# DeltaNet outputs taken by channel with one joint factor, and VectorE's long background operations in pieces, in one hybrid decoder layer

## The chip, the cores and the metric

The kernel runs on one core of one Trainium2 chip. The metric is the device time of one execution, in microseconds (us). Before the change the median of three runs is 1189.47 us (1189.45 to 1190.11).

## The reference: what is computed

One layer over 1024 tokens of width 1024, all in float32. After an RMSNorm one input projection makes the columns of two mixers:

```python
# mixer A, gated DeltaNet: 4 heads of 128; q, k, v pass a causal conv and SiLU, q and k are L2-normed
qa = l2norm(qa) * (GDN_HEAD_DIM ** -0.5)
def step(state, xs):                       # one chunk
    uv, wk, qd, at, ke, ge = xs
    u = uv - wk @ state
    o = qd @ state + at @ u                # qd = gam * q, gam = exp(cumulated log decay)
    state = ge * state + ke.T @ u
    return state, o
o_a = rmsnorm(o_a, gdn_norm_w) * silu(z)   # per token and head, over its 128 channels
# mixer B, dilated attention: 8 heads of 64, three strided bands merged by their softmax denominators
o_b = dilated_attention(qb, kb, vb)
x = x + concat(o_a, o_b) @ w_out
# then RMSNorm, an up-projection to 2 x 2816 columns, conv of width 3, SiLU gate, down-projection, RMSNorm
```

L2-norm and per-token RMSNorm both carry an epsilon of 1e-6. Both scale a token's 128 channels of a head by one number, so the scale of q need not be applied where a normalisation of the output follows, if the epsilon is treated accordingly.

## The kernel before

Activations lie channel by token: 128 channels on the partitions, 1024 tokens in the free dimension. A float32 product is made of three TensorE products of rounded high and low parts (`mm3`: high x high, high x low, low x high, 512 columns each); weights are loaded in tiles of 128x1024 (`wst`), and ScalarE makes the high part (`whi`), VectorE the low part (`wlo`, one operation of 1024 columns).

The program is one list per engine. TensorE's order is fixed when the program is built, by the class `Weave`: streams of work (generators) are started in order of a level, each says how long it must wait by a small cost model, and every matmul gets an order token. The other engines' orders come from a scheduler that follows the dependencies; operations issued through `uv` and `ua` (line 141 in the profile) are put ahead of those through `ve` and `ac` (line 139). Products carry line 192, transposes lines 196 and 201. All engines run their list in order, and DMAs are issued from SP's list, also in order.

The stages, with the times of the profiled execution:

- 0 to 186 us: the first projection columns, norms, and from `dense()` the columns q and v of the four heads (48 products of 512 columns for one column block). For each head `kprep` and `qprep` prepare the chunks. `qprep` transposes qT on TensorE (`tokens`: 8 transposes a head, into PSUM), ScalarE squares each transposed block with an accumulated sum per token (`ssq`), GpSimd raises it to -1/2 (`rq`), and VectorE makes `gq` = gam times rq. VectorE also runs `forward_sub`, the inverses of 32x32 blocks, 31 dependent steps from about 114 to 178 us, whose result goes through DRAM (`xdram`, `xtdram`) to `merges`.
- 186 to 226 us: `merges` joins the inverses to 128x128 blocks, with column blocks of `dense()` between.
- 226 to 303 us: the chain. For each of 4 heads and 8 chunks: product k x state (`ps<-ct,kT`), VectorE makes `r`; product with the inverse (`ps<-r,um`), VectorE makes `wke`, ScalarE `w`; product `ps<-wke,ktok`, VectorE makes the next state `ct`. Then the outputs: `ps<-ct,qat` (q x state) and `ps<-w,qat` (at x w) go token by channel to two halves of a PSUM bank, ScalarE copies one with the scale rq into `vtok`, VectorE adds the other with the scale gq, ScalarE squares the 128x128 block with an accumulated sum `ms`. At a head's end GpSimd raises `ms` to -1/2 and multiplies the 128x1024 `vtok` by it, and `finish(h)` transposes it back on TensorE (8 transposes) and stores it to `mixer`. The heads run interleaved; products of `dense()` (columns of the attention's q, k, v) fill the time between.
- 303 to 460 us: the attention, 4 pairs of heads, again with `dense()` between (the rest of the attention's columns, then the columns z, whose SiLU gates the DeltaNet output `og`, read back from `mixer`).
- 460 to 1188 us: out projection, up-projection, down-projection.

VectorE's operations of `dense()` in the chain and the attention are the eviction of a half column (`aqkv<-ps,rstdB`, 512 columns), the low part of a weight (`wlo<-wst,whi`, 1024 columns) and the 32x32-block transpose of V (`avt<-aqkv`, 1024 columns). Each is one instruction that lies somewhere between the chain's.

Of the kernel before, what the change touches and what calls it, by code (L numbers as in the profile page):

```python
# [7 lines left out]
F32 = mybir.dt.float32  # L8
# [7 lines left out]
P = 128  # L16
# [29 lines left out]
class Weave:  # L46
# [50 lines left out]

    def until(self, name):
        while name not in self.done:
            yield 0.3  # L100
# [20 lines left out]
class Engine:  # L121
# [5 lines left out]
    def __getattr__(self, op):  # L127
        wv, eng, name, fixed, per, lag, first = self.args

        def call(*a, **kw):  # L130
# [9 lines left out]
            with first(offset=URGENT):  # L140
                return getattr(eng, op)(*a, **kw)  # L141
# [3 lines left out]
def hybrid_layer(tc, I, out):  # L145
# [44 lines left out]

    def mm(dst, lhs, rhs, us, start=True, stop=True, **kw):
        tc.stamp_issue_order_token(nc.tensor.matmul(dst, lhs, rhs, start=start, stop=stop, **kw).ins, TOKEN)  # L192
        wv.product(us, dst, lhs, rhs)
# [27 lines left out]
    def weight(src, n=1024, st=None):  # L221
# [4 lines left out]
        lows_made.append(split(st, hi, lo))  # L226
        return hi, lo

    def wk(src, st=None):
        return [t.rearrange("p (k m) -> p k m", k=KT) for t in weight(src, st=st)]  # L230
# [16 lines left out]
    gdram = dp.tile([NCH * H, P], F32, name="gdram")  # L247
    xdram = dp.tile([H, 32, 1024], F32, name="xdram")
# [95 lines left out]
    pick = const("pick", [P, 32])  # L344
    ve.memset(pick, 0.0)
    ve.memset(pick[:, 8:9], 1.0)
# [64 lines left out]
    def gates():  # L411
# [25 lines left out]
        sy.dma_start(gdram, grow)  # L437
        ve.tensor_copy(gc, pt[:, :NCH * H].rearrange("p (c h) -> p c h", c=NCH))
# [5 lines left out]
    def scaled(pair, name, by_class=False, tag="ev", t=None, hs=(0, 1)):  # L444
        if t is None:
            t = A(name, tag)
        for h in hs:
            sl = half(h)
            if by_class:
                ve.tensor_tensor(t[:, sl].rearrange("p (n c u) -> p n u c", n=4, c=4),  # L450
                                        pair[h].rearrange("p (n u c) -> p n u c", n=4, c=4),
                                        rstdB[:, sl].rearrange("p (n u c) -> p n u c", n=4, c=4), op=OP.mult)
# [31 lines left out]
    def gate(og, xr, anchor=None):  # L484
# [3 lines left out]
                 ve.tensor_tensor(og, og, y, op=OP.mult)]  # L488
# [10 lines left out]
    gated = {}  # L499

# [7 lines left out]
    def dense():  # L508
# [7 lines left out]
        raw.append(raw_weight(I["wi"][1]))  # L516
        for i, col in enumerate(DENSE):
# [3 lines left out]
            w = nxt  # L521
            if i + 1 < len(DENSE):
                nxt = wk(None, raw.pop())
# [3 lines left out]
            for hh in range(2):  # L527
                pt = bank("hf")
                yield wv.need(pt, *w)
                for k in range(KT):  # L530
                    mm3(pt, [t[:, k, :] for t in w], [t[:, half(hh)] for t in xs[k]], k == 0, k == KT - 1)
                    yield 0.0

                pair.append(pt)
                if hh == 0:
                    while put_off:
# [12 lines left out]
            elif kind == "z":  # L549
                og = gated[h] = A("og", "kT*")  # L550
                sy.dma_start(og, mixer[h])
                if i + 1 < len(DENSE):
# [3 lines left out]
            else:  # L556
                if col[2] < 2:
                    sy.dma_start(apark[h, col[2]], xr)
                else:
                    t = A("avt", "ev")  # L560
                    ve.transpose(t.rearrange("p (c n j) -> p n c j", c=4, n=NCH), by_block(xr))
                    for b in range(4):
                        sq_.dma_start(avdram[h].rearrange("u x (b j) -> b u x j", b=4)[b],
                                     t[32 * b:32 * b + 32].rearrange("u (x j) -> u x j", j=32))
                wv.done.add(col)
# [20 lines left out]

    def kprep(h):
# [8 lines left out]
        rows = gdram.rearrange("(c h) t -> h c t", h=H)[h]  # L596
        sy.dma_start(v8(dec), bass.AP(tensor=rows.tensor, offset=rows.offset, ap=[[0, P]] + list(rows.ap)))
# [43 lines left out]
    def qprep(h, qT):  # L641
# [3 lines left out]
        ssq = small("ssq")  # L645
        yield from tokens(qT, None, None, ssq)
        ve.tensor_scalar(ssq, ssq, 128.0, 128.0 * EPS, op0=OP.mult, op1=OP.add)
        rq = small("rq", 4)
        rsqrt(rq, ssq, NCH)
# [11 lines left out]
        gq = small("gq", 4)  # L661
# [1126 lines left out]
```

## Time and profile before

| quantity | value |
|---|---|
| median of three runs | 1189.47 us |
| the profiled execution's own time | 1189.92 us |
| its span in the trace | 1188.1 us |
| share of the span that TensorE is busy | 99% |
| share of the span that VectorE is busy | 81% |
| TensorE's idle time, 226 to 303 us (chain) | 1.41 us of 77.00 |
| TensorE's idle time, 303 to 460 us (attention) | 0.39 us of 157.00 |

The span is 1.8 us shorter than the execution's own time; that remainder is taken as unchanged. A row of the timeline gives the start in us, the duration in us, the engine, the line, the operation, the tile written and those read, the size, and in brackets how long the engine had been idle before it and what ended that. Float32 products stand as two records each, transposes as one. Records of TensorE overlap, so the time that an instruction takes is read from one start to the next.

### The profile page before, as it was taken

Reading aid. Unit: us, or ns where it says so; the run is one execution under the profiler, and the core shown is the slowest. Engines: PE = TensorE matmul, PEld = TensorE weight load, DVE = VectorE, ACT = ScalarE, POOL = GpSimd, SP = SyncE. Lnnn points to the kernel's source line nnn. Section 1 sums busy time; section 2 is a strip of 40 time slices with the busy share of each in tenths; the row PEclk is TensorE's granted clock in tenths of the full one; section 3 lists DMA queues with packets and bytes.
Section 4 is the critical chain, followed back from the end, with each engine's and each line's share of the span. In section 5 each row is a group of like instructions: output and inputs, shape, how many; then the busy total and the mean of one; then the engine's idle time right before and its main releaser. Section 6 shows DMA issues by size and latency. Waiting matters only on the chain.

```text
span 1188.1 us, 18252 instructions
## 1 busy us (share of the span) xinstructions
PE 1178.3 (99%) x6994; PEld 975.0 (82%) x6994; DVE 964.0 (81%) x1545; ACT 572.8 (48%) x1122; POOL 54.7 (5%) x49
## 2 busy tenths in 40 slices
PE   9999999999999999999999999999999999999997
PEld 7888888898777778888888888888888888888887
DVE  7786996474577877668998898988889889898987
ACT  7473344364344444545544444545444553546452
POOL 0212001004000000000000000000000000000001
PEclk9999999999999999999999999999999999999999
DMA  7323456727642314443231313122231395356724
GB/s 238 108 94 86 110 141 161 238 96 204 180 141 73 99 37 151 150 151 107 89 99 61 107 54 107 60 100 89 72 106 54 124 379 196 125 178 221 239 96 160
DMA packets 114520, 156.91 MB, mean 132 GB/s; under 512 B 54368, under 2 KB 65408, under 8 KB 114432
## 3 DMA queue, kind: packets, MB, share of 16 engines
q1 hardware_dynamic: 113712, 155.21, 41.3%
q8 instruction: 55, 0.90, 0.3%
q10 hardware_dynamic: 720, 0.53, 0.1%
q14 instruction: 33, 0.27, 0.1%
HBM read 117.68 MB, written 38.03 MB: 131 GB/s over the span
## 4 chain that ended last, share of the span: by engine, by line
PE 98%; DVE 1%; ACT 0%; issue 0%; DVEq 0%; ACTq 0%
PE ps L192 47%; PE pa L192 20%; PE dw L192 18%; PE pc L192 10%; PE ps L201 1%; PE ps L196 1%; PE warm L192 0%; DVE x1h L139 0%; ACT sm L141 0%; PE pd L192 0%; DVE aqkv L139 0%; DVE sm L141 0%; DVE wke L141 0%; DVE xr L139 0%; DVE ct L141 0%
## 5 line engine op out<-in xcount | busy, mean ns | idle before, releaser
L192 PE MATMUL dw<-pr 128*128 128x512 f32 (+1 forms) x984 | 211.4, 377 | 0.0
L192 PEld LDWEIGHTS dw<-pr 128*128 128x128 f32 x984 | 176.7, 188 | 33.7
L192 PE MATMUL ps<-xhi,whi 128*128 128x512 f32 x448 | 184.0, 411 | 0.0
L192 PE MATMUL ps<-xhi,wlo 128*128 128x512 f32 x448 | 175.4, 392 | 0.0
L192 PE MATMUL ps<-xlo,whi 128*128 128x512 f32 x448 | 175.2, 391 | 0.0
L192 PE MATMUL pa<-T,pair 128*128 128x512 f32 x528 | 126.9, 389 | 0.0
L192 PEld LDWEIGHTS pa<-T,pair 128*128 128x128 f32 x528 | 99.1, 188 | 20.6
L192 PEld LDWEIGHTS ps<-xhi,whi 128*128 128x128 f32 x448 | 84.6, 189 | 18.8 <-issue 2.7
L192 PEld LDWEIGHTS ps<-xhi,wlo 128*128 128x128 f32 x448 | 84.3, 188 | 18.2
L192 PEld LDWEIGHTS ps<-xlo,whi 128*128 128x128 f32 x448 | 84.6, 189 | 14.6
L139 ACT ACTIVATE u<-pa 128x512 f32<-128x512 f32 x44 | 26.4, 599 | 114.4 <-PE pa L192 114.4
L139 DVE SCALAR_TENSOR_TENSOR y<-xu,fcw,y 128x1023 f32<-128x1023 f32 (+1 forms) x44 | 56.4, 1281 | 22.1 <-ACT y L139 22.0
L139 ACT ACTIVATE pr<-wd 128x1024 fp32r<-128x1024 f32 x33 | 35.0, 1061 | 72.6 <-DVE wd L139 35.4
L192 PE MATMUL pa<-B,A 128*128 128x512 f32 x264 | 63.5, 390 | 0.0
L192 PE MATMUL pc<-B,pair 128*128 128x512 f32 x264 | 63.4, 389 | 0.0
L192 PE MATMUL pc<-T,S 128*128 128x512 f32 x264 | 63.4, 389 | 0.0
L192 PE MATMUL pa<-T,S 128*128 128x512 f32 x264 | 63.4, 389 | 0.0
L139 ACT ACTIVATE whi<-wst 128x1024 fp32r<-128x1024 f32 (+2 forms) x38 | 38.5, 1013 | 51.1 <-PE ps L192 44.4
L139 DVE TENSOR_TENSOR wst<-wst 128x512 f32<-128x512 f32 x88 | 60.4, 687 | 0.8
L192 PE MATMUL ps<-B,pair 128*128 128x512 f32 x252 | 60.5, 389 | 0.0
L192 PEld LDWEIGHTS pc<-T,S 128*128 128x128 f32 x264 | 49.6, 188 | 10.3
L192 PEld LDWEIGHTS pa<-T,S 128*128 128x128 f32 x264 | 49.6, 188 | 10.3
(248 smaller groups left out, 2217.2 us busy)
## 6 DMA issues: line engine op xcount, KB each, us to landing
wst<-in_wu SPq DMA_DIRECT2D x44, 512.0 KB, 3.6
wd<-in_wd SPq DMA_DIRECT2D x44, 512.0 KB, 4.5
wst<-in_wi SPq DMA_DIRECT2D x25, 512.0 KB, 4.1
upark<-y SPq DMA_DIRECT2D x22, 512.0 KB, 3.5
r<-upark SPq DMA_DIRECT2D x22, 512.0 KB, 10.3
wa<-in_wd SPq DMA_DIRECT2D x22, 256.0 KB, 2.9
apark<-aqkv SPq DMA_DIRECT2D x8, 512.0 KB, 3.3
wst<-in_wo SPq DMA_DIRECT2D x8, 512.0 KB, 3.6
```

The costliest lines, as they stand in the source:

```text
L139: return getattr(eng, op)(*a, **kw)
L192: tc.stamp_issue_order_token(nc.tensor.matmul(dst, lhs, rhs, start=start, stop=stop, **kw).ins, TOKEN)
L196: tc.stamp_issue_order_token(nc.tensor.transpose(dst, src, ident).ins, TOKEN)
L201: tc.stamp_issue_order_token(nc.tensor.transpose(dst, src[rows], ident[rows, rows]).ins, TOKEN)
```

## The change

Four parts:

1. The chain's outputs are computed by channel: `ps<-qat,ct` and `ps<-qat,w` accumulate in one 128x128 PSUM tile (the operands change places), one ScalarE copy puts it into `vtok`, which is now channel by token. The scales rq and gq, the blockwise squares, `ms` with its powers, GpSimd's multiply, the 32 transposes and the 8 copies of `finish(h)` go.
2. q is scaled before the chain by gam alone: `gamdram` holds the rows of gam, one 512 KB load a head spreads them over the partitions, GpSimd multiplies (`qd<-qd,qT`), and qd is parked. The 32 transposes of qT with their squares go; instead ScalarE squares qT in one 128x1024 operation a head, and the squares are parked (`qsqpark`).
3. `finish()` runs once for all heads: ScalarE squares `vtok` (`osq`), GpSimd adds the parked squares of q, 16 TensorE products with a picking matrix sum over the channels, and the sums go through DRAM (`sdram`) to a 128x32 tile `ft`, GpSimd raises that to -1/2, it goes to `fdram`, and one 512 KB load a head (`fB`, one tile for all four) spreads the factors; GpSimd multiplies `og` by them. The gate takes the weight `gw2` along in its last operation.
4. While the chain or the attention runs, VectorE's background operations are cut: an eviction of 512 columns into 2 of 256, a low part of 1024 into 4 of 256, a transpose of 1024 into 4 of 256. They are deferred (`defer`) and placed one by one where the cost model finds VectorE free (`background`), each with order dependencies that put it between two urgent operations.

The diff, cut to its core:

```diff
+    pieces, chains, seen = [], set(), {}
+    def one_piece():
+        _, op, _ = pieces.pop(0)
+        inst = op()
+        if chains:
+            for k in ("urgent", "piece"):
+                if k in seen:
+                    after(inst, seen[k], "the chain's operations lie between")
+            seen["piece"] = seen["new"] = inst
+    def urgent(inst):
+        if chains:
+            if "new" in seen:
+                after(inst, seen.pop("new"), "a piece lies between")
+            seen["urgent"] = inst
+    def background():
+        while "attention" not in wv.done:
+            if pieces and wv.free.get("vector", 0.0) <= wv.pe + 0.05 and wv.need(*pieces[0][2]) <= 0.0:
+                one_piece()
+            yield 0.3
...
-    def weight(src, n=1024, st=None):
+    def weight(src, n=1024, st=None, parts=1):
...
+        ac.activation(hi, st, AF.Copy)
+        for i in range(parts):
+            c = slice(i * n // parts, (i + 1) * n // parts)
+            defer((lo, lambda c=c: ve.tensor_tensor(lo[:, c], st[:, c], hi[:, c].bitcast(F32), op=OP.subtract), [hi]))
...
+        gamrow = tile_(sp, [NCH * H, P], F32, "gamrow", "w0", 1)
+        ac.activation(gamrow, grow, AF.Exp)
+        sy.dma_start(gamdram, gamrow)
...
+                if chains:
+                    defer(*[(pair[h], lambda i=i, f=piece: f(slice(2 * i, 2 * i + 2)), [pair[h]]) for i in range(2)])
...
-                 ve.tensor_tensor(og, og, y, op=OP.mult)]
+                 ve.scalar_tensor_tensor(og, og, gw2, y, op0=OP.mult, op1=OP.mult)]
...
             elif kind == "z":
+                yield from wv.until("f")
                 og = gated[h] = A("og", "kT*")
                 sy.dma_start(og, mixer[h])
+                if not fB:
+                    fB.append(A("fB", "go"))
+                to_all(fB[0], fdram[h])
+                po_.tensor_tensor(og, og, fB[0], op=OP.mult)
...
     def qprep(h, qT):
-        ssq = small("ssq")
-        yield from tokens(qT, None, None, ssq)
-        ve.tensor_scalar(ssq, ssq, 128.0, 128.0 * EPS, op0=OP.mult, op1=OP.add)
-        rq = small("rq", 4)
-        rsqrt(rq, ssq, NCH)
+        qd = A("qd", "qa")
+        to_all(v8(qd), gamdram.rearrange("(c h) t -> h c t", h=H)[h])
...
-        gq = small("gq", 4)
-        ve.scalar_tensor_tensor(gq, ngam[:, :, h], -1.0, rq, op0=OP.mult, op1=OP.mult)
-        sy.dma_start(qpark[h], qT)
+        po_.tensor_tensor(qd, qd, qT, op=OP.mult)
+        sy.dma_start(qpark[h], qd)
+        ac.activation(qT, qT, AF.Square, scale=128.0 * EPS ** 0.5)
+        sy.dma_start(qsqpark[h], qT)
...
             if c:
-                mm(po[:, P:2 * P], qT, st, 0.215)
-            mm(po[:, :P], at, w, 0.215)
-            ua.activation(vtok[:, cs], po[:, :P], AF.Copy, scale=rq[:, c:c + 1])
-            if c:
-                uv.scalar_tensor_tensor(vtok[:, cs], po[:, P:2 * P], gq[:, c:c + 1], vtok[:, cs], op0=OP.mult,
-                                        op1=OP.add)
+                mm(po, st, qT, 0.215, True, False)
+            mm(po, w, at, 0.215, c == 0, True)
+            ua.activation(vtok[:, cs], po, AF.Copy)
...
-            ua.activation(osq, vtok[:, cs], AF.Square, accum_out=ms[:, c:c + 1])
-        uv.tensor_scalar(ms, ms, 1.0 / 128, EPS, op0=OP.mult, op1=OP.add)
-        rsqrt(ms, ms, NCH)
-        po_.tensor_tensor(v8(vtok), v8(vtok), ms[:, :, None].to_broadcast([P, NCH, P]), op=OP.mult)
-        wv.add(1, finish(h, vtok))
-    def finish(h, osb):
-        for hh in range(2):
-            pt = yield from next_bank("atr", osb, slack=0.8)
-            for c in range(4):
-                i = 4 * hh + c
-                tp(pt[:, c * P:(c + 1) * P], osb[:, i * P:(i + 1) * P])
...
+        sy.dma_start(mixer[h], vtok)
+    def finish():
+        for h in range(H):
+            yield from wv.until(("e", h))
+            osq, qsq = A("osq", "kT*"), A("qsq", "kt")
+            osqs.append(osq)
+            sy.dma_start(qsq, qsqpark[h])
+            ac.activation(osq, G[h]["vtok"], AF.Square)
+            po_.tensor_tensor(osq, osq, qsq, op=OP.add)
...
+        for h in range(H):
+            for g in range(4):
+                o = 32 * g
+                mm(pt[o:o + 32, :256], picked(h), by_quarter(osqs[h])[:, g], 0.107, h == 0, h == H - 1,
+                   tile_position=(0, o))
+        sums = tile_(sp, [P, 256], F32, "sums", "t2", 2)
+        ac.activation(sums, pt[:, :256], AF.Identity, scale=1.0 / 128, bias=eps2)
...
+        po_.tensor_tensor(f4, f4, mhalf[:, None, :].to_broadcast([P, 4, NCH]), op=OP.pow)
+        sq_.dma_start(fdram.rearrange(flat, t=32), ft)
+        wv.done.add("f")
```

How the lists of the engines move. First VectorE late in the chain, before the change: an eviction of 512 columns lies ahead of a state (`ct`), and a transpose of 1024 and a low part of 1024 lie in front of an `r`.

```order
L141 SCALAR_TENSOR_TENSOR r<-ps,ngam,vtok 128x128
L139 TENSOR_TENSOR aqkv<-ps,rstdB 128x4x32x4
L141 SCALAR_TENSOR_TENSOR ct<-ct,ge,ps 128x128
L139 STREAM_TRANSPOSE avt<-aqkv 128x8x4x32
L139 TENSOR_TENSOR wlo<-wst,whi 128x1024
L141 SCALAR_TENSOR_TENSOR r<-ps,ngam,vtok 128x128
L141 SCALAR_TENSOR_TENSOR vtok<-ps,gq,vtok 128x128
L141 TENSOR_SCALAR wke<-ps,ke 128x128
```

VectorE in the chain after the change: pieces of a transpose and of a low part, one at a time among the same urgent operations.

```order
L142 STREAM_TRANSPOSE avt<-aqkv 128x2x4x32
L144 SCALAR_TENSOR_TENSOR ct<-ct,ge,ps 128x128
L142 STREAM_TRANSPOSE avt<-aqkv 128x2x4x32
L144 SCALAR_TENSOR_TENSOR ct<-ct,ge,ps 128x128
L144 SCALAR_TENSOR_TENSOR r<-ps,ngam,vtok 128x128
L142 TENSOR_TENSOR wlo<-wst,whi 128x256
L144 SCALAR_TENSOR_TENSOR r<-ps,ngam,vtok 128x128 x3
L142 TENSOR_TENSOR wlo<-wst,whi 128x256
L144 TENSOR_SCALAR wke<-ps,ke 128x128
L142 TENSOR_TENSOR wlo<-wst,whi 128x256
L144 TENSOR_SCALAR wke<-ps,ke 128x128 x3
L144 SCALAR_TENSOR_TENSOR ct<-ct,ge,ps 128x128
```

What moved: no instruction of over 256 columns stands ahead of an urgent one there, the second operation of an output (`vtok<-ps,gq,vtok`) is gone, and the pieces stand one by one.

Second GpSimd from the preparation of q to the chain, after the change (`xi` is the tile in which `forward_sub` works, `x` those into which the inverses are loaded).

```order
L142 TENSOR_TENSOR qd<-qd,qT 128x1024
L142 MEMSET xi 128x1024
L142 AFFINE_SELECT xi<-xi 128x1024
L142 TENSOR_TENSOR qd<-qd,qT 128x1024 x2
L142 MEMSET x_1663 128x1024
L142 MEMSET x_1677 128x1024
L142 TENSOR_TENSOR qd<-qd,qT 128x1024
```

What moved: before, the powers of 128x8 (`rq`) stood in place of the multiplies, and the two operations that make `xi` stood ahead of all of them; now the first multiply stands ahead of `xi`, and two more lie between `xi` and the tiles of the inverses.

Third SP's queue behind the end of the chain, after the change: the way of the joint factor, and what is queued behind it (V and K of the attention's third pair, and the weights `wst` of a column block).

```order
L142 DMA ft_3048<-sdram_85 128x32
L142 DMA fdram_86<-ft_3048 128x32
L142 DMA fB_4347<-fdram_86 128x1024
L142 DMA fB_4347<-fdram_86 128x1024
L142 DMA mixer_80<-oT_3295 128x512
L142 DMA avdram_90<-avt_3167 1024x1x32
L142 DMA avdram_90<-avt_3167 1024x1x32 x3
L142 DMA fB_4347<-fdram_86 128x1024
L142 DMA wst_3431<-in_wi 128x1024
L142 DMA kT_3643<-apark_89 128x1024
L142 DMA fB_4347<-fdram_86 128x1024
```

What moved: none of the five factor rows was there before; the first fB loads stand before what follows, and a load of the one fB tile waits for GpSimd's multiply with its content before.

On TensorE 27 of `dense()`'s products of 512 columns stand further ahead: 744 instead of 717 of them come before the first product of the merges (`ps<-x,um`), and 975 before the attention, as before. The runs of such products that follow products of another kind are 83 instead of 91.

130 lines of the change are left out of this document (102 added, 28 removed).

## The prediction

> **What bounds the kernel now.** I read the page first, then the windows by stage, then the view of waits, and then single rows around each place that the change touches.
>
> ```profile
> span 1188.1 us, 18252 instructions
> PE 1178.3 (99%) x6994; PEld 975.0 (82%) x6994; DVE 964.0 (81%) x1545; ACT 572.8 (48%) x1122; POOL 54.7 (5%) x49
> PE 98%; DVE 1%; ACT 0%; issue 0%; DVEq 0%; ACTq 0%
> ```
>
> TensorE is busy 1178.3 of 1188.1 us, and 98% of the chain that ended last is TensorE's own work. So there are two currencies. A product or transpose taken off TensorE's list is worth its full time from start to start. Everything else counts only where TensorE stands idle, now or afterwards. The idle time of the two stages in which VectorE's order is changed bounds what the pieces can bring:
>
> ```profile
> 226.00:303.00 77.00, 75.59 (x490) 67.73 (x489) 43.98 (x127) 38.14 (x139) 15.96 (x12) 1.00 0.55 171
> 303.00:460.00 157.00, 156.61 (x1705) 120.17 (x1705) 120.03 (x334) 69.48 (x210) 3.64 (x8) 1.00 0.34 99
> ```
>
> The first number behind the comma is TensorE's busy time: idle are 1.41 us in the chain and 0.39 us in the attention. The granted clock is 1.00 in both, so no number here has to be scaled by it. VectorE is busy 44 of 77 us in the chain and 120 of 157 us in the attention: it is not short of time there, only an instruction can lie in front of an urgent one.
>
> **TensorE's own work: 4.7 us less.** The transposes that go:
>
> ```profile
> L196 PE MATMUL ps<-ident,vtok 128*128 128x128 f32 x32 | 4.7, 273 | 0.0
> L196 PE MATMUL ps<-ident,qT 128*128 128x128 f32 x32 | 4.1, 272 | 0.0
> ...
> 299.23 1.03 PE L196 MATMUL ps<-ident,vtok 128*128 128x128 f32 x8
> 300.01 0.48 PE L192 MATMUL ps<-xhi,whi 128*128 128x512 f32 x1
> 300.33 0.40 PE L192 MATMUL ps<-xlo,whi 128*128 128x512 f32 x1
> 300.56 0.39 PE L192 MATMUL ps<-xhi,wlo 128*128 128x512 f32 x1
> ```
>
> The records overlap, so I take starts: 8 transposes occupy 300.01 - 299.23 = 0.78 us. Both groups have the same mean (273 and 272 ns), so 64 of them are 8 x 0.78 = 6.24 us. The first product of 512 columns behind a group of another kind costs 300.33 - 300.01 = 0.32 us instead of 300.56 - 300.33 = 0.23, and the order shows 83 instead of 91 such changes: 8 x 0.09 = 0.72 us less.
>
> What is added are 16 picking products of 32x256. The kernel has four of the same shape in its norms:
>
> ```profile
> 29.14 0.64 PE L192 MATMUL ps<-acc,pick 128*32 128x256 f32 x8
> 29.71 0.50 PE L192 MATMUL ps<-xhi,whi 128*128 128x512 f32 x1
> ```
>
> Eight records are four instructions (float32 products stand as two); they take 0.57 us, so 16 take 2.28 us. The chain's two output products only change their operands' places, same sizes and number. Sum: -6.24 - 0.72 + 2.28 = **-4.7 us**. All of it lies on the path.
>
> **Waits that the pieces can remove: 2.1 us.** The view of waits for the chain, and one of the places:
>
> ```profile
> PE ps L192 <- DVE ct L141: 0.9, 2, 0.5
> PE ps L192 <- ACT w L141: 0.5, 1, 0.5
> ...
> 252.42 1.05 DVE L139 TENSOR_TENSOR aqkv<-ps,rstdB 128x512 f32<-128x512 f32 x1
> 252.66 0.39 PE L192 MATMUL ps<-w,qat 128*128 128x128 f32 x2
> 252.89 0.39 PE L192 MATMUL ps<-r,um 128*128 128x128 f32 x2
> 253.33 0.31 DVE L141 SCALAR_TENSOR_TENSOR ct<-ct,ge,ps 128x128 f32<-128x128 f32 x1
> 253.70 0.49 PE L192 MATMUL ps<-ct,kT 128*128 128x128 f32 x2 [0.42 <-DVE ct L141]
> ```
>
> An eviction of 512 columns holds `ct`, and TensorE loses 0.42 us by the bracket; start to start it is 253.70 - 252.89 = 0.81 us where the product ahead of it took 252.89 - 252.66 = 0.23, so 0.6. By this the 1.4 us of the view are 2.0 us at most. The piece that replaces the eviction is half as long, so it can still hold the state, for half the time; and the outputs' second operation (28 of `vtok<-ps,gq,vtok`) is gone from VectorE's list. I take **-1.8 us** (bounds 0 and -2.0). In the attention all idle is 0.39 us; there the last link is the softmax's own division. I take **-0.3** (bounds 0 and -0.4).
>
> The pieces cost VectorE time, from these rows:
>
> ```profile
> L139 DVE TENSOR_TENSOR wlo<-wst,whi 128x1024 fp32r<-128x1024 f32 x33 | 40.3, 1220 | 7.4 <-ACT whi L139 7.3
> L139 DVE TENSOR_TENSOR wlo<-wst,whi 128x384 fp32r<-128x384 f32 x2 | 1.1, 560 | 3.2 <-ACT whi L139 3.2
> ```
>
> (1220 - 560) / 640 = 1.03 ns a column, and 0.16 us that every instruction has: 256 columns take 0.43 us, four of them 1.7 instead of 1.22. Over nine weights, 14 evictions and three transposes that is about 9 x 0.5 + 14 x 0.16 + 3 x 0.5 = 8.2 us more, spread over stages where VectorE is idle 33 + 37 us, less 9.7 us of outputs' operations. It is covered; if it were not, a late `wlo` would stall TensorE by its own lateness.
>
> **New: the start and the end of the inverses.** In the preparation of q VectorE is saturated, and `forward_sub` runs in it as one dependent line that the merges wait for:
>
> ```profile
> 95.63 0.95 POOL L139 MEMSET xi<- 128x1024 f32 x1
> 96.66 1.27 POOL L139 TENSOR_SCALAR_AFFINE_SELECT xi<-xi 128x1024 f32<-128x1024 f32 x1
> ...
> 107.54 1.06 ACT L139 ACTIVATE qT<-qT 128x1024 f32<-128x1024 f32 x1
> ...
> 114.30 0.19 DVE L139 TENSOR_TENSOR tmp<-mt,xi 128x31 f32<-128x31 f32 x1 [1.50 <-DMA mt<-mdram]
> 177.85 1.13 DVE L139 COPY mt<-xi 128x1024 f32<-128x1024 f32 x1
> 193.13 1.99 SPq L139 DMA_DIRECT2D x<-xdram  x4
> 196.90 2.21 PE L192 MATMUL ps<-x,um 32*32 32x32 f32 x128
> 266.64 1.90 POOL L139 TENSOR_TENSOR vtok<-vtok,ms 128x1024 f32<-128x1024 f32 x1
> x<-xdram SPq DMA_DIRECT2D x8, 64.0 KB, 2.3
> ```
>
> Before, `xi` was ready at 97.9. Now GpSimd's first multiply of q stands ahead of it, and that waits for the SiLU of q, at 108.6; with 1.9 us for the multiply (as the one at 266.64, of the same size) and 2.2 for the two operations on `xi`, the tile is ready between 112.7 and, if gam's rows come late, some 116: 0 to 2 us behind the 114.30 at which the first step started. The loads of the inverses were issued until 195.1 and landed 2.3 us later at about 197; the merges started at 196.90. So there was no margin. Now the merges come later on TensorE: 27 products of 512 columns more (27 x 0.23 = 6.2) less 32 transposes with their changes (3.5) give 2.7 us. The delay against it: 0 to 2 us at the start, 1.5 us of VectorE's operations that stand ahead of the copy now and did not before, and what two multiplies of GpSimd take from VectorE (0 to 3.8 us, see the rivals); VectorE's idle spots in this stretch take back up to 2 us. The result is between nothing and some 3.5 us of new wait. I take **+0.7 us**, nearer to nothing, since most of the terms have to come together.
>
> ScalarE loses 32 squares with their sums and 8 copies and gets 8 operations of 128x1024; it was busy 38 of the chain's 77 us, which hides them. SP issues 19 DMAs more; between the inverses' stores and loads stands a load of gam's rows where the store of q stood.
>
> **New: the joint factor.** Its rows, by the nearest kin:
>
> ```profile
> L139 POOL TENSOR_TENSOR ms<-ms,mhalf 128x8 f32<-128x8 f32 x4 | 6.5, 1636 | 14.1 <-DVE ms L141 14.0
> L139 POOL TENSOR_TENSOR rs<-rs,mhalf 128x2 f32<-128x2 f32 x1 | 0.7, 695 | 13.6 <-DVE rs L139 13.6
> dec<-gdram SPq DMA_DIRECT2D x4, 512.0 KB, 7.8
> ```
>
> A power takes 0.16 us a column and 0.38 besides, so 128x32 takes 5.4 us. Around it lie three passages through DRAM of 2.3 to 7.8 us each and a broadcast like that of `dec` for each head. From the picks on that is 13 to 29 us to the first fB, and with 1.9 us and another load for each further head 40 to 50 us to the last one. SP's list stands behind it, as the order shows, with K and V of the attention's third pair and the weights of the columns z. The columns z start 165 of `dense()`'s products behind the picks, 38 us of them alone; the attention holds 369 of these, 84 of its 157 us, so 38 us stretch to 70. The third pair starts some 60 us behind the picks (two pairs of four in 157 us, less the picks' own place 15 us into the first). So 10 us are left, and I put it at 0. When they are used up, each further us is one of TensorE's.
>
> For GpSimd's multiplies against the softmax, tight links of the chain, which the order shows closer together than before, and anything unseen I take **+0.7 us** (0 to 7.6).
>
> **Sum.** -4.7 - 1.8 - 0.3 + 0.7 + 0.7 = -5.4 us. Against the profiled execution's own 1189.92 us, whose span is 1188.1, that is 1184.5; the median of the runs is 0.45 lower, so **1184.0 us**.
>
> **Rivals.** Slower: **GpSimd's multiplies hold VectorE.** The rows that bear on it:
>
> ```profile
> 268.17 0.86 DVE L141 TENSOR_SCALAR ms<-ms 128x8 f32<-128x8 f32 x1 [0.38 <-ACT osq L141]
> 279.00 0.17 DVE L141 TENSOR_SCALAR ms<-ms 128x8 f32<-128x8 f32 x1 [0.95 <-ACT osq L141]
> 116.48 2.77 POOL L139 TENSOR_TENSOR rq<-ssq,mhalf 128x8 f32<-128x8 f32 x1 [18.55 <-DVE ssq L139]
> ```
>
> A VectorE operation of 0.17 us took 0.86 when it met the multiply at 266.64. Against that, a power of 1.64 us took 2.77 amid VectorE's dense work: there it was GpSimd that waited. The change has 12 such multiplies instead of 4. Two fall into `forward_sub`, whose operations read two tiles in SBUF each, and four into the attention's divisions. If each holds VectorE for its whole 1.9 us, the inverses come 3.5 us late and the divisions 4 x 1.9 = 7.6: 11.1 us against 6.8 saved, 1194 us. It decides from 9 of these 11 us on, and less than half gives no difference worth the name.
>
> [...]
>
> **No difference: half of that.** With 1.5 us at the inverses, 2 us at the divisions and one more for the factor the gain shrinks to 2.3 us, about 1187.5. **Larger gain:** all waits of both stages go and no new ones come: -4.7 - 2.0 - 0.4 = -7.1, 1182.4. **The change doesn't do what it says:** the pieces still meet the urgent operations, as any order made from a cost model may; then only TensorE's own -4.7 and the +1.4 stay: 1186.2, still faster.
>
> **Numbers.** Chances: the forecast 0.45, the larger gain 0.15, the pieces without effect 0.15, no difference 0.14, slower 0.11. What a measurement of this kernel can tell from no change is about 0.2%, 2.4 us. So faster has 0.75, same 0.14, slower 0.11. The range goes from 1180.8 (the larger gain, and 1.6 us for idle time that the brackets understate) to 1189.0 (into the case of no difference).
>
> **What would show it.** Right: the first `ps<-x,um` starts 2.7 us later than before, with no bracket; 16 picks in 2.3 us; less than 0.5 us of idle time in the chain; the stages behind the attention as long as before. Wrong: a bracket on the first `ps<-x,um` that names a DMA (the inverses late), divisions of the softmax of over 1 us beside `og<-og,fB`, or weights late behind fB.

## The result, and the profile after

| | before | after | ratio |
|---|---|---|---|
| median of 11 runs, us | 1189.97 (1189.23 to 1190.29) | 1186.77 (1185.72 to 1187.99) | 0.9975, 95% interval 0.9966 to 0.9984 |
| profiled execution, us: own time / span | 1189.92 / 1188.1 | 1187.61 / 1185.0 | |

The changed kernel's profiled execution is 2.6 us longer than its span, not the 1.8 us that were taken as unchanged; its other ten runs lie at 1.8 to 1.9. So below span is compared with span: 3.1 us.

The change makes the kernel 3 us faster, a quarter of a percent. The direction was forecast, and the time lies in the range, but 5.4 us were forecast: more than two of them are missing. The page of the changed kernel:

```profile
span 1185.0 us, 18118 instructions
PE 1173.8 (99%) x6962; PEld 969.6 (82%) x6962; DVE 968.7 (82%) x1556; ACT 555.4 (47%) x996; POOL 65.8 (6%) x50
```

TensorE is busy 4.5 us less (1178.3 before), and the span is only 3.1 us shorter. So TensorE's own work went about as forecast, and new waits ate part of it. The windows of chain and attention say where:

```profile
226.00:303.00 77.00, 76.69 (x516) 67.78 (x518) 42.47 (x130) 28.13 (x82) 11.37 (x8) 1.00 0.63 198
303.00:460.00 157.00, 154.02 (x1707) 117.49 (x1700) 124.32 (x352) 66.18 (x201) 18.53 (x13) 1.00 0.40 119
```

Idle time in the chain fell from 1.41 to 0.31 us. In the attention it rose from 0.39 to 2.98 us. TensorE's rows with a bracket in that window, of the changed kernel (TensorE's timeline):

```profile
335.64 0.71 PE L242 MATMUL ps<-ident,sm 64*128 64x64 f32 x16 [1.44 <-DVE sm L144]
336.55 0.73 PE L242 MATMUL ps<-ident,sm 64*128 64x64 f32 x16 [0.20 <-DVE sm L144]
...
397.45 1.09 PE L233 MATMUL ps<-kT,qT 64*128 64x256 f32 x5 [0.59 <-ACT pb L144]
...
412.31 0.60 PE L242 MATMUL ps<-ident,sm 64*128 64x64 f32 x8 [0.57 <-DVE sm L144]
```

Four waits, 2.80 us together; the kernel before has none of them. The first two have a neighbour on GpSimd. VectorE's timeline at that place, then the same divisions in VectorE's timeline of the kernel before, and then GpSimd's of the changed kernel:

```profile
333.06 2.77 DVE L144 TENSOR_SCALAR sm<-sm,mx 128x416 f32<-128x416 f32 x2
335.76 0.15 DVE L144 RECIPROCAL mx<-mx 128x2 f32<-128x2 f32 x1
335.94 0.82 DVE L144 TENSOR_SCALAR sm<-sm,mx 128x448 f32<-128x448 f32 x2
```

```profile
336.81 0.78 DVE L141 TENSOR_SCALAR sm<-sm,mx 128x416 f32<-128x416 f32 x2
```

```profile
326.28 2.38 POOL L142 TENSOR_TENSOR og<-og,fB 128x1024 f32<-128x1024 f32 x1 [5.28 <-DMA fB<-fdram]
...
332.88 2.37 POOL L142 TENSOR_TENSOR og<-og,fB 128x1024 f32<-128x1024 f32 x1 [3.75 <-DMA fB<-fdram]
339.66 2.38 POOL L142 TENSOR_TENSOR og<-og,fB 128x1024 f32<-128x1024 f32 x1 [4.40 <-DMA fB<-fdram]
346.69 2.39 POOL L142 TENSOR_TENSOR og<-og,fB 128x1024 f32<-128x1024 f32 x1 [4.65 <-DMA fB<-fdram]
```

The pair of divisions of 416 columns starts 0.18 us behind the second multiply and takes 2.77 us (0.78 before); the pair of 448 columns right behind, larger and with no multiply beside it, takes 0.82. The divisions end at 335.83, 0.6 us after the multiply. The others held VectorE as well: four pieces of a low part took 3.51 us beside the first (1.42 in x1 below, without multiplies) and a pair of divisions of 128 columns 0.79 us beside the third (0.48). A pair of 288 columns that begins as the fourth ends took 1.14 us (0.65), with a memset of GpSimd beside it. But TensorE has no bracket behind any of these.

What the rest of the program did, from the same rows in both traces: the merges start at 199.50 (196.90 before), the chain takes 61.68 us to its last product instead of 65.59, and the 16 picks take 1.87 us (302.52 to 304.39). TensorE's timeline of the changed kernel:

```profile
199.50 2.21 PE L233 MATMUL ps<-x,um 32*32 32x32 f32 x128
...
302.52 1.93 PE L233 MATMUL ps<-osq,picks 128*32 128x256 f32 x32
304.39 0.50 PE L233 MATMUL ps<-xhi,whi 128*128 128x512 f32 x1
```

### The profile page after: what moved, and what is told of

Its sections match the earlier page's. It is cut to its first block, busy times and chain, and to the rows that moved or that the text cites. A ratio compares the mean times of both kernels' runs of the same rounds, so it can differ in the third digit from the quotient of the medians.

```text
span 1185.0 us, 18118 instructions
## 1 busy us (share of the span) xinstructions
PE 1173.8 (99%) x6962; PEld 969.6 (82%) x6962; DVE 968.7 (82%) x1556; ACT 555.4 (47%) x996; POOL 65.8 (6%) x50
## 4 chain that ended last, share of the span: by engine, by line
PE 96%; DVE 2%; SPq 1%; ACT 1%; DMA 0%; issue 0%; DVEq 0%; ACTq 0%
PE ps L233 46%; PE pa L233 20%; PE dw L233 18%; PE pc L233 10%; PE ps L242 1%; SPq L142 1%; DVE sm L144 1%; PE ps L237 1%; PE warm L233 0%; DMA wst<-in_wi 0%; DVE wlo L142 0%; DVE x1h L142 0%; ACT sm L144 0%; PE pd L233 0%; DVE pt L144 0%
## 5 line engine op out<-in xcount | busy, mean ns | idle before, releaser
L142 DVE TENSOR_TENSOR wlo<-wst,whi 128x256 fp32r<-128x256 f32 (+3 forms) x65 | 50.9, 802 | 15.6 <-ACT whi L142 15.6
L144 ACT ACTIVATE sm<-sm,mx 128x128 f32<-128x128 f32 (+7 forms) x64 | 35.4, 555 | 51.6 <-DVE mx L144 51.6
```

The source lines that it names most:

```text
L144: inst = getattr(eng, op)(*a, **kw)
```

## The experiments

Two theories were set against each other for the missing time. **A:** GpSimd's multiplies by the factor hold VectorE's divisions. **B:** the waits come from VectorE's pieces and their order in the attention. Later **C** took B's place: the order that the cost model makes with the pieces, TensorE's too, leaves two places of the attention without cover. Each ratio is that of the kernel's runs to those of the kernel before in the same set of runs.

| run | median, us | before, us | ratio (95% interval) |
|---|---|---|---|
| x1 without the multiplies | 1185.24 | 1189.95 | 0.9957 (0.9945 to 0.9970) |
| x2 no pieces | 1193.72 | 1189.95 | 1.0031 (1.0016 to 1.0045) |
| x3 pieces in the chain alone | 1190.51 | 1189.95 | 1.0006 (0.9998 to 1.0015) |
| x4 kernel before, with pieces | 1190.47 | 1189.95 | 1.0004 (0.9995 to 1.0013) |
| x5 two multiplies for one | 1197.31 | 1189.92 | 1.0051 (1.0034 to 1.0069) |
| x6 multiply in the gate | 1187.98 | 1189.92 | 0.9984 (0.9975 to 0.9992) |
| x7 multiply on VectorE | 1187.72 | 1189.92 | 0.9982 (0.9973 to 0.9990) |
| x8 0.6 us more allowance | 1196.48 | 1189.92 | 1.0056 (1.0044 to 1.0068) |
| x9 quarters, last gate lost | 1188.00 | 1189.90 | 0.9983 (0.9974 to 0.9992) |
| x10 0.2 us more allowance | 1186.15 | 1189.90 | 0.9968 (0.9956 to 0.9981) |
| x11 both, last gate lost | 1188.29 | 1189.90 | 0.9987 (0.9979 to 0.9996) |
| x12 quarters | 1186.13 | 1189.48 | 0.9970 (0.9959 to 0.9981) |
| x13 quarters and 0.2 us | 1184.69 | 1189.48 | 0.9960 (0.9946 to 0.9973) |
| x14 no multiplies and 0.2 us | 1184.16 | 1189.48 | 0.9954 (0.9941 to 0.9966) |

**x1, the multiplies left out.**

```diff
-                po_.tensor_tensor(og, og, fB[0], op=OP.mult)
```

> The changed kernel without GpSimd's four multiplies of og by fB (the joint factor is left out of the result; its sums, its power and the loads of fB stay). Theory A: a multiply of 2.4 us holds VectorE's softmax divisions (the pair of divisions at 333.06 took 2.77 us, TensorE waited 1.44 + 0.20 behind it), so without them these 1.6 us go and the kernel takes about 4.7 us less than the one before (1185.2). Theory B: the waits in the attention come from VectorE's pieces and their order, and the multiply only shifts them: no more than 3.2 us less than before (1186.8), with TensorE still idle some 3 us in the attention.

Measured: 4.7 us less than before, as A said. TensorE's list is the same as in the changed kernel; the waits of 1.44 and 0.20 are gone, and those of 0.59 and 0.57 stand unchanged. So the multiplies cost about 1.6 us by the brackets (the intervals of the two ratios overlap a little, from 0.9966 to 0.9970), and they are not all that is missing.

**x2, x3, x4: where the pieces act.** x2 never defers, x3 drops the one line that keeps the pieces going in the attention, and x4 gives the pieces to the kernel before:

```diff
-                nxt = wk(None, raw.pop(), 4 if chains else 1)
+                nxt = wk(None, raw.pop())
-                if chains:
+                if False:
...
-        chains.add("attention")
```

> The changed kernel with VectorE's background operations whole, never deferred; all else as changed. Theory A: the chain's waits of 1.4 us by the brackets come back (1.4 to 2.0 us), the attention's stay, so only 1.2 to 1.8 us less than before (1188.4). Theory B: the chain's waits come back, but the later waits of the attention (0.59 at 396.9, 0.57 at 411.7 and what the brackets leave out) go: about 2.7 us less than before (1187.2).

> The changed kernel with pieces in the chain alone and whole background operations in the attention. Theory A: as the changed kernel, 3.2 us less than before (1186.8), since the multiplies hold VectorE either way. Theory B: the attention's later waits go, 4.4 us less than before (1185.6).

> The kernel before with the pieces alone (deferred and ordered as in the change), outputs and finishing as before. Theory A: the chain's waits go, 1.4 to 2.0 us less than before (1188.2). Theory B: the pieces cost in the attention what they save in the chain: within 0.5 us of before. If the pieces do nothing at all in this chain, the brackets of 0.4 to 0.5 us on ct and w stay.

Neither theory had x2 and x3 right: without pieces the change is 3.7 us slower than the kernel before, and with pieces in the chain alone it is no faster. In x2 three sets of divisions met a multiply. GpSimd's timeline of x2, then VectorE's, then TensorE's:

```profile
327.59 2.37 POOL L142 TENSOR_TENSOR og<-og,fB 128x1024 f32<-128x1024 f32 x1 [5.91 <-DMA fB<-fdram]
```

```profile
327.87 3.10 DVE L144 TENSOR_SCALAR sm<-sm,mx 128x384 f32<-128x384 f32 x2
```

```profile
330.78 0.63 PE L242 MATMUL ps<-ident,sm 64*128 64x64 f32 x12 [1.70 <-DVE sm L144]
331.35 0.50 PE L233 MATMUL ps<-xhi,whi 128*128 128x512 f32 x1
331.68 0.39 PE L233 MATMUL ps<-xlo,whi 128*128 128x512 f32 x1
...
332.14 0.63 PE L233 MATMUL ps<-xhi,whi 128*128 128x512 f32 x1
332.57 0.63 PE L233 MATMUL ps<-xlo,whi 128*128 128x512 f32 x1
```

A pair of divisions of 384 columns takes 3.10 us there; in the changed kernel, where no multiply meets it, it takes 0.75. And something shows that neither theory had: from 332.14 on a product of 512 columns takes 0.43 us from start to start instead of 0.23, for some three and a half microseconds. TensorE's granted clock was 0.50 from 332.1 to 335.5 (more on it at the end), so this wait cost more than its bracket. In x2 this happened behind two waits. The profiled execution is the slowest of x2's eleven (1197.75 us, mean granted clock 0.995); the fastest took 1190.20 us at 0.998, so a good part of the median's loss goes with the clock.

By the medians the pieces are worth nearly 7 us in the changed kernel. Part of that is what they were made for. x2's chain has 1.70 us of waits again and is 2.3 us longer, after taking off three products of 512 columns that now lie in it. In x3 the longest wait, 2.47 us at 447.32, stands behind a whole low part of 1024 columns (445.38), which lies ahead of a softmax's divisions and itself waited 2.15 us for `whi`; the last multiply was over 96 us before, and the clock is halved for 3.4 us behind that wait. The rest comes by accident: the pieces shift which instruction a multiply meets, and how long it is.

x4 is the cleanest of the three, and its time is what theory B said. Against the kernel before, its chain is 1.7 us shorter (63.90 instead of 65.59 us to the last product, of which 0.7 are three products of 512 columns that moved behind it); the waits on `ct` are gone, while that on `w` stays (0.47 us) and a second one comes (0.34). Then the attention loses it all. TensorE's timeline of x4, and then of the kernel before:

```profile
399.60 0.96 PE L242 MATMUL ps<-ident,sm 64*128 64x64 f32 x24
401.14 1.08 PE L233 MATMUL ps<-kT,qT 64*128 64x256 f32 x5 [0.58 <-ACT pb L144]
```

```profile
399.67 0.96 PE L201 MATMUL ps<-ident,sm 64*128 64x64 f32 x24
400.56 0.50 PE L192 MATMUL ps<-xhi,whi 128*128 128x512 f32 x1
...
402.84 1.89 PE L192 MATMUL ps<-kT,qT 64*128 64x256 f32 x40
```

The bracket of 0.58 is the changed kernel's at 397.45, in a kernel with no multiply at all. TensorE's list explains it: in the kernel before nine products of 512 columns stand between these transposes (`ident,sm`) and the scores (`kT,qT`); in x4 and in the changed kernel none does. The wait belongs to the pieces, through TensorE's order. That is theory C. The wait of 0.57 a step later is in x4 as well (0.57 at 415.9). There the list of TensorE is the same, and VectorE is late: in the changed kernel three pieces and an eviction stand ahead of the softmax, which starts at 409.42, 1.57 us behind its scores at 407.85; before, it started 0.52 us behind them (413.26 and 412.74). VectorE's timeline of the changed kernel there, and then the softmax's start in that of the kernel before:

```profile
407.82 1.09 DVE L142 TENSOR_TENSOR wlo<-wst,whi 128x256 fp32r<-128x256 f32 x3
408.82 0.68 DVE L142 TENSOR_TENSOR xr<-ps,rstdB 128x512 f32<-128x512 f32 x1
409.42 0.28 DVE L144 CUSTOM_DVE_ANT_0 sm<-ps,mk 128x128 f32<-128x128 f32 x1
```

```profile
413.26 0.29 DVE L141 CUSTOM_DVE_ANT_0 sm<-ps,mk 128x128 f32<-128x128 f32 x1
```

**x5, x6, x7: dose, place and engine of the multiply.**

```diff
+                po_.tensor_tensor(fB[0], fB[0], og, op=OP.mult)                                  # x5, behind the first
...
-                po_.tensor_tensor(og, og, fB[0], op=OP.mult)                                     # x6, in gate()
+                 po_.tensor_tensor(y, y, fB[0], op=OP.mult),
...
-                po_.tensor_tensor(og, og, fB[0], op=OP.mult)                                     # x7
+        flush(og)                                                                                # x7, in gate()
+                defer(*[(og, lambda c=slice(256 * i, 256 * i + 256), og=og: ve.tensor_tensor(og[:, c], og[:, c], fB[0][:, c], op=OP.mult), [og, fB[0]]) for i in range(4)])
```

> The changed kernel with every multiply of og by fB followed by a second GpSimd multiply of the same size (into fB, which is loaded anew afterwards, so the result is the same). TensorE's order is unchanged. Theory A (the multiply holds VectorE): more divisions and pieces meet a multiply, some 1.5 us more wait, 1.6 us less than before instead of 3.1 (1188.4). Theory B (the wait at the divisions has another cause, or comes only with the first multiply): no change from 1186.8.

> The changed kernel with GpSimd's multiply by fB moved into the gate: it takes the gate's own intermediate, which VectorE makes behind a softmax's divisions, so that it starts when these are over. Same number, size and engine, TensorE's order unchanged; result as the reference's. Theory A: no multiply meets a division, the wait of 1.44 + 0.20 goes, 4.7 us less than before as without the multiplies (1185.2), unless VectorE waits in its list for the product. Theory B: 3.1 us less (1186.8).

> The changed kernel with the multiply by fB on VectorE, in four pieces of 256 columns a head among the other pieces. Theory A: no GpSimd operation with inputs in the attention, so the wait goes; 16 pieces of 0.43 us are 6.9 us of VectorE, in a stage where it is idle 33 us, but each may stand ahead of an urgent operation: 4.0 to 4.7 us less than before (1185.6). Theory B: 3.1 us less or worse (1187).

x5 went A's way, but by far more than the 1.5 us that were expected: by the ratios 9 us more than with one multiply. VectorE's timeline of x5 shows a hold on two-input pieces as well as on divisions:

```profile
338.50 4.45 DVE L142 TENSOR_TENSOR wlo<-wst,whi 128x256 fp32r<-128x256 f32 x2
...
363.85 4.25 DVE L144 TENSOR_SCALAR sm<-sm,mx 128x352 f32<-128x352 f32 x2
```

Two pieces of 256 columns take 4.45 us (0.75 where no multiply runs), two divisions 4.25. TensorE waits 2.35 + 0.56 us behind the first and 1.53 + 1.14 behind the second, and the clock halves after both. The clock is most of the surplus: in the profiled execution it is halved for 13.7 us, which costs about 6.8. Six of x5's seven runs took 1195.25 to 1198.10 us at mean granted clocks of 0.992 to 0.995, and the seventh 1189.03 us at 0.997, close to the 1188.4 us that were expected.

x6 and x7 take the hold off the divisions and gain nothing. In x6 the wait at 335 is gone, but the first multiply, from 403.32 to 405.71, now meets three pieces, and the gate's operation (1.27 us at 406.59) stands behind them. VectorE's timeline of x6:

```profile
404.56 2.11 DVE L142 TENSOR_TENSOR wlo<-wst,whi 128x256 fp32r<-128x256 f32 x3
...
460.71 1.29 DVE L142 SCALAR_TENSOR_TENSOR og<-og,gw,zz 128x1024 f32<-128x1024 f32 x1 [2.57 <-POOL zz L142]
```

The softmax behind them is late (1.02 + 0.58 us of wait on TensorE, where the changed kernel has 0.57), and at the end of the attention VectorE itself waits 2.57 us for GpSimd. In x7 an eviction lies between the divisions and the last step waits 0.75 + 0.79, with half the clock for 3.4 us behind it. x6 misses both theories' numbers; x7's time is theory B's case (3.1 us less or worse), though no multiply runs on GpSimd. The traces settle it and not the times: the wait at 335 is gone in both, and the repair put as much on VectorE's list as it took away.

**x8 and x10: cover.** More allowance in the two waits that place the scores and the transposes in TensorE's list:

```diff
-TSLACK = -1.0, -0.6
+TSLACK = -0.4, -0.6            # x8; x10: -0.8
...
-            yield wv.need(*pair[0]["ps"], *pair[1]["ps"], pair[0]["q"], pair[0]["k"])
+            yield wv.need(*pair[0]["ps"], *pair[1]["ps"], pair[0]["q"], pair[0]["k"], slack=0.6)       # x8 alone
```

> The changed kernel, but the order of TensorE is made with 0.6 us more allowance ahead of the scores and of the transposes of probabilities, so that more of the 512-column products stand ahead of each. Theory C: the two later waits of the attention (0.59 on ACT pb at 396.9, 0.57 on DVE sm at 411.7), which the kernel with the pieces alone has too, are places where the order made with the pieces left no cover: they go, 4.2 us less than before (1185.8), the wait behind the multiply stays. Rival: the cover taken there is missing at the end of the attention, and the gain is under 0.5 us.

> The changed kernel with 0.2 us more allowance ahead of the transposes of the probabilities alone. TensorE's order then has 9 products of 512 columns between transposes and scores at the place of the wait of 0.59 (before this change too there were 9; with the pieces none), and 24 of them behind the last values instead of 42. Theory C: the wait of 0.59 on ACT pb goes, that of 0.57 perhaps too: 3.7 to 4.2 us less than before (1186.0). Rival: the wait reappears where the cover was taken, no gain or worse, as with the larger allowance (x8).

x8 is its rival's case, and worse: the cover is spent before the last transposes, where TensorE waits 6.83 us, and the clock is halved for 13.7 us. x10 removes the waits of 0.59 and 0.57 from the trace and moves part of them to the end of the attention (one of 1.07 us on an eviction). 0.6 us are left of the gain against the changed kernel's 1186.77, hardly more than the two medians can tell.

**x9, x11 to x14: how long a hold lasts, and whether the causes add up.**

```diff
-                po_.tensor_tensor(og, og, fB[0], op=OP.mult)
+                for j in range(4):
+                    cs = slice(256 * j, 256 * j + 256)
+                    po_.tensor_tensor(og[:, cs], og[:, cs], fB[0][:, cs], op=OP.mult)
```

> The changed kernel with each GpSimd multiply of og by fB cut into four of 256 columns (some 0.6 us each); TensorE's order is unchanged and the result is the same. Theory A (VectorE is held for the whole of the instruction that it meets): a pair of divisions is held some 0.6 us at a time instead of up to 2, the wait of 1.44 + 0.20 shrinks to under 0.5, 4.3 us less than before (1185.6). Rival A2 (the two engines share a bandwidth, so that the sum of the work counts): the divisions are as slow beside four pieces as beside one multiply, 3.1 us less (1186.8).

> Both edits, multiplies in quarters and 0.2 us more allowance. If the two causes are separate their gains add up: 4.9 to 5.4 us less than before (1184.8), which is what was forecast for the change. If only theory A holds, 4.3 us less; if neither, 3.1.

> The changed kernel with each GpSimd multiply of og by fB in four of 256 columns, everything else and TensorE's and VectorE's lists as in the changed kernel. Theory A (VectorE is held for the whole of the one instruction that it meets): the divisions are held 0.7 us at most, the wait behind them falls from 1.64 to 0.3 to 0.5 us, 4.2 us less than before (1185.7). Rival A2 (the hold is of the work, however it is cut): 3.1 us less or worse (1186.8).

> Quarters and 0.2 us more allowance ahead of the transposes of probabilities. If the two causes are separate and all that is missing: 4.9 to 5.4 us less than before (1184.8). Rival: the end of the attention, where 24 instead of 42 products of 512 columns are left, gives new waits on VectorE (in x10 one of 1.07 us), so 4.0 us less or worse.

> Without the multiplies (the joint factor is left out of the result) and with 0.2 us more allowance: the bound of what the two edits can bring. If both causes are separate: 5.3 us less than before (1184.6). If the allowance only moves its waits to the end of the attention: as without the multiplies alone, 4.7 to 5.1 us less.

x9 and x11 named the loop variable as the outer loop's and so left out the last head's gate, which also changed VectorE's list at the end of the attention (waits of 0.75 to 2.31 us there); their times say nothing of the quarters. x12 and x13 are the same edits with the gate. VectorE's timeline of x12, at the second multiply (which now meets the pair behind that of 416 columns) and at the third:

```profile
334.20 1.38 DVE L144 TENSOR_SCALAR sm<-sm,mx 128x448 f32<-128x448 f32 x2
...
341.30 1.64 DVE L144 TENSOR_SCALAR sm<-sm,mx 128x256 f32<-128x256 f32 x2
```

The longest hold of a pair is now about 1.0 us, on average half a microsecond for each of its two instructions (1.64 instead of 0.62), where a whole multiply held one for 2. For a single instruction that is as theory A has it: a hold within the 0.73 us of one quarter there, not the 2.90 us of all four. But the four quarters take 2.90 to 3.36 us, some 3.1, instead of 2.4 and meet more instructions. Summed over the four multiplies, by the rows of x1 as the undisturbed durations, VectorE is held some 4.6 us in x12 and 4.9 in the changed kernel; in this A2 is right. The brackets only fall from 1.64 to about 1.1 us, and the gain against the kernel before is 3.4 instead of 3.2 us, where theory A expected 4.2.

x13 gives 4.8 us less than before (0.9960), x14 5.3 (0.9954), both close to what was expected. So without the multiplies and with a little more cover the time is what was forecast for the change, 5.4. The ratios' intervals of x1, x10 and x12 to x14 overlap, though, so the medians alone don't show that the gains add up.

The traces show it better. Take the stretch from the chain's last output product to the first product of the up-projection (`pa<-B,A`): 255.31 us before. TensorE's list has 27 products of 512 columns and 8 transposes less there and 16 picks more, 5.1 us by the prices above, so 250.2 us would be no loss. One execution each:

| us | multiplies whole | in quarters | left out |
|---|---|---|---|
| allowance as in the change | 253.63 (changed kernel) | 253.48 (x12) | 251.79 (x1) |
| 0.2 us more | 252.39 (x10) | 251.95 (x13) | 250.77 (x14) |

Leaving the multiplies out takes off 1.8 and 1.6 us, the allowance 1.2, 1.5 and 1.0, each nearly whatever the other is; the quarters only 0.2 and 0.4. The pieces alone (x4) lose 1.6 us in this stretch, as much as x1 still does. So the two causes are separate, and together they are 2.9 of the 3.4 us that the changed kernel loses here. x13 leaves nothing out of the result; all of its five runs (1184.24 to 1185.69) lie below the changed kernel's eleven, though from another set, in which the kernel before was 0.5 us faster too.

## Why the prediction was half right

- **TensorE's own work, -4.7:** right. The page has 4.5 us less. By TensorE's rows the merges come 2.60 us later, where 27 products more and 32 transposes less were to make 2.7, and the picks took 1.87 us instead of 2.28.
- **The waits in the chain, -1.8:** nearly right. The chain is 3.91 us shorter with the same 117 products of 512 columns in it, of which 24 transposes are 2.3; at most 1.6 are left for the waits, and the idle time fell by 1.1. x4 shows that the pieces take the waits on `ct`; those on `w` go only with the outputs by channel (x2, which has these without pieces, has none).
- **The start and end of the inverses, +0.7:** nothing was lost, but by luck. The delay was there: VectorE's copy came at 181.63 (177.85 before), 3.8 us late. One multiply held `forward_sub` itself for 2.1 us (below), the next a low part that stood ahead of it (2.50 us at 161.03 instead of 1.22). The last load of the inverses was issued at 196.87; its landing is not recorded, but with the 2.3 us of before it is an estimated 199.2, and the merges started at 199.50 without a bracket. So the 2.7 us by which the merges moved were just enough. In the runs with the same first part the merges start between 198.96 and 200.47, so a few tenths of this are chance. VectorE's timeline of the changed kernel, and then of the kernel before:

```profile
133.64 2.48 DVE L142 TENSOR_TENSOR tmp<-mt,xi 128x240 f32<-128x240 f32 x1
...
181.63 1.13 DVE L142 COPY mt<-xi 128x1024 f32<-128x1024 f32 x1
```

```profile
134.12 0.41 DVE L139 TENSOR_TENSOR tmp<-mt,xi 128x240 f32<-128x240 f32 x1
```

- **The joint factor, 0:** right. The power took 5.4 us as worked out, and none of TensorE's waits in the attention ended with a transfer.
- **The step that failed: "For GpSimd's multiplies against the softmax, tight links of the chain ... and anything unseen I take +0.7 us (0 to 7.6)", and with it the -0.3 of the attention.** The mechanism was the rival's, and its size lay between the forecast and the rival. x1 prices the multiplies at 1.6 us, and all of it comes from one of the four. The prediction had the row that bears on it (an operation of 0.17 us that took 0.86), and still took a tenth of the bound. The other 1.2 us were not among its terms: that the pieces change TensorE's order in the attention and put VectorE behind at one softmax (x4). The order showed the first, transposes and scores with nothing between them; the prediction had compared TensorE's orders only as far as the attention's start. Together -0.3 + 0.7 became +2.8 by the brackets. With 4.5 us less of TensorE's work, 1.1 us less idle time in the chain and 2.6 us more in the attention the whole comes to -3.0, against 3.1 us of span. The 0.7 us at the inverses, which did not come, hid part of the miss.
- **"The pieces without effect":** as a rival it was wrongly built. x2 shows the change without pieces 3.7 us slower than before, not 3.3 faster: three pairs of divisions meet a multiply (waits of 1.70, 1.48 and 0.92 + 0.38 us), the clock is halved behind two of them, and 1.70 us of waits in the chain are back.

What the rows show of a hold: the step of `forward_sub` at 133.64, which has two inputs in SBUF, began 0.30 us behind a multiply (133.34, 2.53 us) and took 2.48 us instead of 0.41, until 0.25 us after the multiply's end. In x12 the longest hold of a pair came to about 0.5 us an instruction, beside quarters of 0.73. The divisions, which have one full tile as input, were held too (2.77 us for a pair of 0.78). VectorE's operations of the chain with an input in PSUM were not: beside GpSimd's adds of 2.38 us (at 267.92 and 272.99) those of 128x128 took 0.34 to 0.35 us, as elsewhere in the chain.

## What to carry to other kernels

An engine that is busy 6% of the time (GpSimd, 65.8 us) cost the bottleneck engine some 1.6 us here, because one of its instructions, of 2.37 us, held a pair of divisions in an urgent queue (2.77 us instead of 0.78). Count the meetings, not the load, and ask of each what the bottleneck has to do meanwhile: at least three of the four multiplies held VectorE, and TensorE waited behind one. And where an order is made by a cost model, a change to one engine's background work is a change of every engine's order: compare the orders to the end of the last stage that the model plans, above all for places where cover has gone. Here a single meeting gave back the chain's whole gain of 1.6 us.

## What the runs showed of the hardware

**TensorE's clock halved behind some waits.** In windows of 1 or 2 us around waits in x2, x3, x5, x7 and x8 the granted clock was 1.00 or 0.50, with mixed values at the switch. Behind the single wait of 1.70 us in x2 (with light transposes before and after it) it was 0.50 from 332.1 to 335.5; behind 0.92 + 0.38 us in x2 from 352.6 to 356.0; behind 2.35 + 0.56 us in x5 from 345 to 351.9; in x8, from within the wait of 6.83 us on, from 448 to 461.7. Behind 1.44 + 0.20 us in the changed kernel's profiled execution it stayed 1.00, and behind 1.48 us in x2 too, so the length of the wait alone does not decide. At half the clock the products took 0.43 us instead of 0.23, so the 3.4 us of it behind x2's first wait cost some 1.7, as much as the wait itself. The half clock came in portions: worked out from the clocks of the windows of 1 and 2 us it lasted 3.40 to 3.44 us each time in x2 (twice), x3 and x7, 6.84 us each time in x5 (twice) and 13.64 us in x8, which is about one, two and four times 3.4. So even the shortest of these cost some 1.7 us. TensorE's timeline of x5:

```profile
344.71 0.49 PE L242 MATMUL ps<-ident,sm 64*128 64x64 f32 x4 [2.35 <-DVE sm L144]
345.76 0.74 PE L242 MATMUL ps<-ident,sm 64*128 64x64 f32 x8 [0.56 <-DVE sm L144]
...
347.45 0.63 PE L233 MATMUL ps<-xhi,wlo 128*128 128x512 f32 x1
347.87 0.63 PE L233 MATMUL ps<-xhi,whi 128*128 128x512 f32 x1
```

Some of the spread of the times goes with the clock: the two slowest of the changed kernel's eleven runs (1187.99 and 1187.73 us) have a mean granted clock of 0.996, the others 0.997 or 0.998. Where it halved in those two no trace shows.

**GpSimd's multiplies with two full inputs took 2.37 to 2.58 us** for 128x1024 in the changed kernel (`og<-og,fB` 2.37 to 2.39, `qd<-qd,qT` 2.38 to 2.58), where the prediction had taken 1.90 from one whose second input is repeated from 8 columns.
